# A fused encoder block on one core: operand tiles of the projections, gates and output projection placed 32 or 68 bytes apart

## The chip, the core and the metric

The kernel runs on one core of a Trainium2 chip. The metric is the time of one execution of the program on the device, in microseconds (us). Before the change three runs took 2656.34, 2660.68 and 2661.32 us; the median is 2660.68 us. The profiled execution, from which all rows below are taken, took 2661.26 us; its span from the first to the last instruction is 2659.4 us.

Engines are named as in the profile: PE is TensorE's matmuls, PEld its loads of the stationary operand, DVE VectorE, ACT ScalarE, POOL GpSimd, SP SyncE, which issues DMAs.

## The reference, cut to what matters

One layer, 2048 tokens, model width 1024, all in float32:

```python
n = rms_norm(h, g_mix)
z = n @ w_in + b_in                         # 1024 x 5120
q, k, v, u, bg, cg, ga, gc = split(z)       # 512 512 512 512 512 512 1024 1024
ya = chunked_rel_attention(q, k, v, ...)    # 8 heads x 64, bands of 576 keys
yc = bg * (conv_b + sum_j conv_w[j] * shift(cg * u, 2 - j))
m = sigmoid(ga) * (ya @ w_pa) + sigmoid(gc) * (yc @ w_pc)
h = h + m @ w_o
n2 = rms_norm(h, g_ffn)
h = h + hier_moe(n2, ...)                   # top group of 4, then top 2 of 8 SwiGLU experts
gate = sigmoid(rms_norm(h, g_ple) @ w_ple_gate + b_ple_gate)
h = h + gate * (p @ w_ple_proj)
```

## The kernel before

**Split products.** Every large product is made of three matmuls. An operand X is split into a high part, a rounded copy (`split`, line 79, on ACT), and a low part, X minus the high part (line 80, on DVE or POOL). `mm3` (lines 82 to 92) then issues, for each slice of 128 of the contraction, three matmuls into the same PSUM tile: stationary high with moving high (line 90), stationary high with moving low (line 91), stationary low with moving high (line 92). Each matmul is preceded by a load of its 128 x 128 stationary slice, so that the program on PE is a chain load, matmul, load, matmul. A stationary slice is 128 float32 of a partition, 512 bytes; a moving operand is 512 columns, 2048 bytes, or 256 columns, 1024 bytes.

**The stages, in order of time.** Stage 1 (0 to about 570 us) makes q, k and v of four heads at a time and, between their matmuls, the attention of earlier tiles. There the weights `wh`, `wl` (`load_w`, from line 161) are the moving operands, 512 columns for q and k and 256 for v, and the normalised tokens `nh`, `nl` the stationary ones. The weights of each half of the heads are 8 pairs of tiles, which stay for 16 tiles of tokens. Stage 2 (to about 1600 us) goes over four blocks of 512 tokens. For each it loads the tokens (`load_n`, 8 pairs `nh`, `nl`, moving), and streams the weights in chunks `whi`, `wlo` (stationary) through the projections u, C and B and the gates; `yh`, `yl` and `ych`, `ycl` are the moving operands of the products with w_pa and w_pc. `gate` gives 8 pairs `mh`, `ml`, which are stationary in the output projection (`out_proj`), where the chunks are the moving operand. Stage 3 (1630 to 2427 us) is the mixture of experts: gathered tokens `xAh`, `xAl`, `xB` and activations `aAh`, `aAl`, `aB` are stationary, weight chunks move. Stage 4 (2456 to 2655 us) is the last gate: `xh`, `xl` stationary, chunks `whi`, `wlo` and one pair `w7h`, `w7l` moving, 512 columns each, and for the last tile partly 256.

**Where tiles lie.** A pool lays its tiles out in a partition's memory one behind the other, each from a multiple of 32 bytes on; `bufs=8` under one name makes 8 equal buffers. Pools on the left start behind the constants of `setup`, whose last tile is a `pad`; pools on the right start from the other end. In this text the *place* of a tile is its first byte modulo 512. Since 128 float32 are 512 bytes and 512 columns are 2048, all slices of a tile that `mm3` uses begin at the place of the tile, and a moving operand also ends where the next row of 512 bytes has this place. *Place apart* is the place of the moving operand of a matmul less that of the stationary slice that is loaded for the next matmul while it runs.

The order of instructions on each engine is set by the order in which the code issues them; pools set which instruction waits for which buffer.

Of the kernel before, what the change touches and what calls it, by code (L numbers as in the profile page):

```python
# [7 lines left out]
F32 = mybir.dt.float32  # L8
F32R = mybir.dt.float32r
# [64 lines left out]
class K:  # L74
# [21 lines left out]
    def setup(self, ctx):  # L96
        tc, nc, a = self.tc, self.nc, self.a
        self.cst = c = ctx.enter_context(tc.tile_pool(name="cst", bufs=1))
        self.dr = d = ctx.enter_context(tc.tile_pool(name="dr", bufs=1, space=DRAM))
        self.ident = c.tile([128, 128], F32, name="ident")  # L100
        make_identity(nc, self.ident)
        self.identr = c.tile([128, 128], F32R, name="identr")
        nc.vector.tensor_copy(self.identr, self.ident)
        self.H = d.tile([S, D], F32, name="H")
        self.N2 = d.tile([S, D], F32, name="N2")
        self.Y = d.tile([2 * S + (NE + MAXOV) * CAP, D], F32, name="Y")
        self.PP = d.tile([S, D], F32, name="PP")
        self.mhalf = c.tile([128, 8], F32, name="mhalf")
        nc.vector.memset(self.mhalf, -0.5)
        self.NTd = d.tile([128, 8, S], F32, name="NTd")  # L110
        self.YAT = d.tile([128, 4, S], F32, name="YAT")
        self.banks, self.nbank = [], 0

        c.tile([128, 88], F32, name="pad")

    def bank(self, dt=F32):
        self.nbank += 1
# [9 lines left out]
    def stage1(self, outer, after, lead=11, lag=2):  # L127
        tc, nc, a = self.tc, self.nc, self.a
        with ExitStack() as ctx:
# [4 lines left out]
            pj = pjx.enter_context(tc.tile_pool(name="s1proj", bufs=2, side="right", reuse_waits="tile"))  # L134
# [25 lines left out]
            def load_w(g, ks):  # L160
                b = a["w_in"]
                for k in ks:
                    if g == 0:
                        raw = early[:, k - 4, 0:768] if k > 3 else att.tile([128, D], F32, name="QT", bufs=4)[:, 0:768]
                    else:
                        raw = pj.tile([128, D], F32, name="xt", bufs=3)[:, 0:768]
                    self.wlast = nc.sync.dma_start(raw.rearrange("p (s c) -> p s c", c=256),
                                      bass.AP(tensor=b.tensor, offset=b.offset + k * 128 * 5120 + g * 256,
                                              ap=[[5120, 128], [512, 3], [1, 256]]))
                    wh = pj.tile([128, 768], F32R, name="wh", bufs=8)  # L170
                    wl = pj.tile([128, 768], F32R, name="wl", bufs=8)
                    self.split(raw, wh, wl)
                    W[g, k] = (wh, wl)

# [64 lines left out]
            def proj(g, t):  # L239
# [4 lines left out]
                for half in range(2):  # L244
                    if g == 1 and t == 0:
                        load_w(g, range(4 * half, 4 * half + 4))
                    ks = range(4 * half, 4 * half + 4)
                    self.mm3(pqk, st[4 * half:4 * half + 4], [(W[g, k][0][:, 0:512], W[g, k][1][:, 0:512]) for k in ks], 4 * half, 8)
                    if half == 0:
                        yield  # L250
# [233 lines left out]
    def stage2(self, outer, inner):  # L484
# [30 lines left out]
        with ExitStack() as ctx:  # L515
            rctx = ctx.enter_context(ExitStack())
            rt = rctx.enter_context(tc.tile_pool(name="s2right", bufs=2, side="right", reuse_waits="tile"))
            bank = self.bank
            one = lambda shape, name: rt.tile(shape, F32, name=name, bufs=1)
            small = one([128, 128], "small")  # L520
            bT = small[:, 0:28]
            nc.scalar.dma_start(bT, a["b_in"][0, 1536:5120].rearrange("(c p) -> p c", p=128))
            cw = small[:, 28:40].rearrange("p (j c) -> p j c", j=3)
# [10 lines left out]
            def load_n(b):  # L534
                out = []
                for k in range(8):
                    raw = rt.tile([128, 512], F32, name="nraw")
                    nc.scalar.dma_start(raw, self.NTd[:, k, 512 * b:512 * b + 512])
                    hi = rt.tile([128, 512], F32R, name="nh", bufs=8)
                    lo = rt.tile([128, 512], F32R, name="nl", bufs=8)  # L540
                    self.split(raw, hi, lo)
                    out.append((hi, lo))
                return out
# [12 lines left out]
            def proj_T(ch, n, k0=0):  # L556

                ps = bank()
                K_ = len(n)
                st = [(ch[0][:, (k0 + k) * 128:(k0 + k + 1) * 128], ch[1][:, (k0 + k) * 128:(k0 + k + 1) * 128]) for k in range(K_)]  # L560
                self.mm3(ps, st, n, 0, K_)
                return ps
# [24 lines left out]
            def gate(c, n, ya, yc):  # L587
                pga = proj_T(self.chunk(), n)
                sa = two.tile([128, 512], F32, name="sa")
                nc.scalar.activation(sa, pga, AF.Sigmoid, bias=bT[:, 12 + c:13 + c])  # L590
                pgc = proj_T(self.chunk(), n)
                sc = two.tile([128, 512], F32, name="sc", bufs=1)
                nc.scalar.activation(sc, pgc, AF.Sigmoid, bias=bT[:, 20 + c:21 + c])
                ch = self.chunk()
                pa = proj_T(ch, ya)
                nc.vector.tensor_mul(sa, sa, pa)
                pc = proj_T(ch, yc, 4)
                nc.vector.tensor_mul(sc, sc, pc)  # L598
                nc.gpsimd.tensor_tensor(sa, sa, sc, op=ALU.add)  # L599
                hi = two.tile([128, 512], F32R, name="mh", bufs=8)  # L600
                lo = two.tile([128, 512], F32R, name="ml", bufs=8)
                self.split(sa, hi, lo)
                return hi, lo

# [155 lines left out]

            YC = []
            n = load_n(0)
            for c in range(4):
                for _ in conv(0, c, n):
# [3 lines left out]
            two = ctx.enter_context(tc.tile_pool(name="s2left", bufs=2, reuse_waits="tile"))  # L768
# [525 lines left out]
    def stage4(self, out):  # L1294
        tc, nc, a = self.tc, self.nc, self.a
        with ExitStack() as ctx:
            two = ctx.enter_context(tc.tile_pool(name="s4two", bufs=2, reuse_waits="tile"))
# [22 lines left out]
            def add(t, ys, h):  # L1320
                nc.vector.scalar_tensor_tensor(h, ys[0], self.WT[0][:, t:t + 1], h, op0=ALU.mult, op1=ALU.add)
                nc.vector.scalar_tensor_tensor(h, ys[1], self.WT[1][:, t:t + 1], h, op0=ALU.mult, op1=ALU.add)
# [53 lines left out]
            self.split_scaled(*w7, self.gple[:, 7:8])  # L1376
            WP = [self.chunk(6 - k) for k in range(7)] + [w7[1:]]
            order.close()
            two.tile([128, 48], F32, name="pad", bufs=1)
            add(todo[0], *ld[0][:2])  # L1380
            xs = turn(ld[0][1])
            r = norm(*ld[0][:2])
# [63 lines left out]
```

## Time and profile before

| | |
|---|---|
| median of three runs | 2660.68 us |
| profiled execution, its span | 2661.26 us, 2659.4 us |
| PE busy, share of the span, matmuls | 2595.2 us, 98%, 13313 |
| loads of the stationary operand (PEld) busy | 2184.5 us, 82% |
| DVE, ACT, POOL busy | 63%, 50%, 32% |
| granted TensorE clock, mean | 0.992 of full |

How to read the rows. The row of an engine on the page gives busy time, share of the span and instructions. A view by windows gives for each stretch its length, the busy time of each engine with the number of instructions, the granted TensorE clock, the share of the DMA engines and what they moved. A row of a group of instructions gives line, engine, operation, output<-inputs by the names in the code (stationary and moving in alphabetical order), the shapes, how many, the busy time in us and the mean duration of one in ns, and the idle time just before them. A row of the order of time gives the start in us, the duration, and the same names; a row with x4 stands for four in a run. Matmuls overlap in the profile: one starts well before the end of the one before it, so what a matmul costs is the distance from its start to the next start, here called the pace; in a settled chain the duration shown is the pace and about 162 ns.

### The profile page before, as it was taken

The page shows a single profiled execution, that of the slowest core. Times are in us where ns is not written, and L with a number is a line of the kernel's source. Part 1 is how long each engine was busy: PE and PEld are TensorE (multiplying, and loading weights), DVE is VectorE, ACT ScalarE, POOL GpSimd, SP SyncE. Part 2 cuts the span into 40 slices and gives each one's busy share as a digit, 9 for nine tenths or more (in the row PEclk, how much of TensorE's full clock was granted, in tenths as well). Part 3 has the DMA queues.
Part 4 walks back from the last instruction along what each step waited for, and adds up shares of the span by engine and source line. Part 5 has one row for each costly group of instructions (what it writes and reads, how often), then busy time and mean ns, then how long its engine had stood idle before and what let it go on. Part 6 is the DMA issues. An engine that isn't in the chain of part 4 may idle for free.

```text
span 2659.4 us, 36515 instructions
## 1 busy us (share of the span) xinstructions
PE 2595.2 (98%) x13313; PEld 2184.5 (82%) x13313; DVE 1675.8 (63%) x2399; ACT 1341.6 (50%) x2025; POOL 841.0 (32%) x681
## 2 busy tenths in 40 slices
PE   7999999999999999999999998999999999998999
PEld 6898888878888888888888886888888888886887
DVE  7778867775444445444445446777777678775654
ACT  5666755564333323332333224766666666665322
POOL 2655465510000100010001003544554555542222
PEclk9999999999999999999999998999999999998999
DMA  5222311044335334533453346888989889987553
GB/s 185 72 68 60 110 48 41 9 129 137 102 128 189 103 95 143 170 102 95 137 170 103 95 151 210 307 309 295 315 304 313 302 314 309 312 309 258 207 187 103
DMA packets 349623, 465.11 MB, mean 175 GB/s; under 512 B 26240, under 2 KB 222080, under 8 KB 349440
## 3 DMA queue, kind: packets, MB, share of 16 engines
q1 hardware_dynamic: 314944, 388.35, 44.8%
q0 software_dynamic: 12096, 43.00, 4.3%
q10 hardware_dynamic: 22400, 31.41, 3.5%
q8 instruction: 105, 1.72, 0.3%
q14 instruction: 78, 0.64, 0.1%
HBM read 400.30 MB, written 62.39 MB: 174 GB/s over the span
## 4 chain that ended last, share of the span: by engine, by line
PE 84%; DVE 6%; DMA 4%; issue 3%; POOL 1%; ACT 1%; SPq 0%; another core or an unknown queue 0%; DVEq 0%; POOLq 0%; ACTq 0%
PE acc L90 22%; PE acc L92 22%; PE acc L91 22%; PE acc L1039 4%; PE acc L1040 4%; PE big L348 2%; PE big L380 2%; DMA h<-H 1%; DMA wraw<-w 1%; PE acc L393 1%; PE acc L394 1%; PE acc L1008 1%; PE acc L674 1%; PE acc L294 1%; POOL g L1362 1%
## 5 line engine op out<-in xcount | busy, mean ns | idle before, releaser
L80 DVE TENSOR_TENSOR wlo<-wraw,whi 128x1024 fp32r<-128x1024 f32 x464 | 694.5, 1509 | 478.4 <-ACT whi L79 465.3
L79 ACT CAST whi<-wraw 128x1024 fp32r<-128x1024 f32 x560 | 585.8, 1053 | 777.8 <-PE acc L91 375.6
L90 PE MATMUL acc<-nh,whi 128*128 128x512 f32 x896 | 349.7, 392 | 2.0 <-ACT nh L79 2.0
L91 PE MATMUL acc<-nl,whi 128*128 128x512 f32 x896 | 350.0, 391 | 0.0
L92 PE MATMUL acc<-nh,wlo 128*128 128x512 f32 x896 | 348.8, 389 | 0.0
L80 POOL TENSOR_TENSOR wlo<-wraw,whi 128x1024 fp32r<-128x1024 f32 x96 | 238.1, 2480 | 123.4 <-ACT whi L79 115.8
L599 POOL TENSOR_TENSOR sa<-sa,sc 128x512 f32<-128x512 f32 x32 | 41.3, 1290 | 538.3 <-DVE sc L598 493.2
L90 PE MATMUL acc<-whi,xAh 128*128 128x512 f32 x512 | 204.1, 399 | 0.4 <-ACT xAh L1011 0.4
L91 PE MATMUL acc<-wlo,xAh 128*128 128x512 f32 x512 | 200.1, 391 | 0.0
L92 PE MATMUL acc<-whi,xAl 128*128 128x512 f32 x512 | 200.0, 391 | 0.0
L90 PEld LDWEIGHTS acc<-nh,whi 128*128 128x128 f32 x896 | 168.1, 188 | 37.2 <-ACT nh L79 2.7
L92 PEld LDWEIGHTS acc<-nh,wlo 128*128 128x128 f32 x896 | 168.3, 188 | 34.5
L91 PEld LDWEIGHTS acc<-nl,whi 128*128 128x128 f32 x896 | 168.3, 188 | 33.4
L90 PE MATMUL acc<-wh,nh 128*128 128x512 f32 (+1 forms) x512 | 176.6, 346 | 0.3 <-ACT wh L79 0.2
L91 PE MATMUL acc<-wl,nh 128*128 128x256 f32 (+1 forms) x512 | 174.1, 341 | 2.1 <-DVE wl L80 2.1
L92 PE MATMUL acc<-wh,nl 128*128 128x256 f32 (+1 forms) x512 | 174.5, 342 | 0.0
L385 ACT CAST PTh<-big 128x640 fp32r<-128x640 f32 (+4 forms) x128 | 80.3, 628 | 85.7 <-PE big L380 84.3
L367 ACT ACTIVATE L<-L,mn 128x640 f32<-128x640 f32 (+4 forms) x128 | 98.4, 769 | 38.2 <-DVE mn L365 15.1
L90 PEld LDWEIGHTS acc<-whi,xAh 128*128 128x128 f32 x512 | 96.5, 189 | 20.8 <-ACT xAh L1011 1.0
L92 PEld LDWEIGHTS acc<-whi,xAl 128*128 128x128 f32 x512 | 96.3, 188 | 20.5 <-DVE xAl L1012 0.2
L1039 PE MATMUL acc<-whi,xB 128*128 128x512 f32 x288 | 112.9, 392 | 0.0
L1040 PE MATMUL acc<-wlo,xB 128*128 128x512 f32 x288 | 112.2, 390 | 0.0
(328 smaller groups left out, 5918.1 us busy)
## 6 DMA issues: line engine op xcount, KB each, us to landing
wraw<-w SPq DMA_DIRECT2D x384, 512.0 KB
wraw<-w_in SPq DMA_DIRECT2D x112, 512.0 KB
wraw<-w_o SPq DMA_DIRECT2D x32, 512.0 KB
y<-Y SPq DMA_DIRECT2D x32, 512.0 KB
xt<-x SPq DMA_DIRECT2D x16, 512.0 KB
xt<-NTd SPq DMA_DIRECT2D x16, 512.0 KB
nraw<-NTd ACTq DMA_DIRECT2D x32, 256.0 KB
wraw<-w_pa SPq DMA_DIRECT2D x32, 256.0 KB
```

What stands on the lines that cost most here:

```text
L79: (hi_eng or self.nc.scalar.copy)(hi, raw)
L80: (lo_eng or self.nc.vector).tensor_sub(lo, raw, hi.bitcast(F32))
L90: self.nc.tensor.matmul(ps, sh, mh, start=first, stop=False)
L91: self.nc.tensor.matmul(ps, sh, ml, start=False, stop=False)
L92: mm = self.nc.tensor.matmul(ps, sl, mh, start=False, stop=last)
L348: nc.tensor.matmul(big[:, 512 * c:512 * c + hi - lo], QT[g, t][:, s, h * 128:(h + 1) * 128], KT[0][:, h, ks:ks + hi - lo], start=(s == 0), ...
L367: nc.scalar.activation(L[:, :n], L[:, :n], AF.Exp, bias=mn, scale=-1.0, accum_out=sm)
L380: nc.tensor.transpose(pt[:, j * 128:(j + 1) * 128], L[:, j * 128:(j + 1) * 128], self.ident)
L385: nc.scalar.copy(hi, ptv)
L599: nc.gpsimd.tensor_tensor(sa, sa, sc, op=ALU.add)
L1039: nc.tensor.matmul(ps, st, ch[0][:, sl], start=first, stop=False)
L1040: nc.tensor.matmul(ps, st, ch[1][:, sl], start=False, stop=last)
```

## The change

No operation, DMA or wait is taken out or put in. In stage 1 and 2 the names of operand tiles get a number, so that each of 8 pairs has tiles of its own with one buffer instead of one of 8 buffers of a common name; each tile is 8 float32 wider than what is used of it, so that the next one begins 32 bytes further on. The tiles `mh`, `ml` are in addition used from element c on, so that successive pairs are 68 bytes apart. The pad behind the constants gets 256 bytes smaller, and so does the tile `small`; a pad in stage 4 goes.

```diff
-        c.tile([128, 88], F32, name="pad")
+        c.tile([128, 24], F32, name="pad")
...
-                    wh = pj.tile([128, 768], F32R, name="wh", bufs=8)
-                    wl = pj.tile([128, 768], F32R, name="wl", bufs=8)
+                    wh = pj.tile([128, 776], F32R, name=f"wh{k}", bufs=1)[:, 0:768]
+                    wl = pj.tile([128, 776], F32R, name=f"wl{k}", bufs=1)[:, 0:768]
...
-            small = one([128, 128], "small")
+            small = one([128, 64], "small")
...
-                    hi = rt.tile([128, 512], F32R, name="nh", bufs=8)
-                    lo = rt.tile([128, 512], F32R, name="nl", bufs=8)
+                    hi = rt.tile([128, 520], F32R, name=f"nh{k}", bufs=1)[:, 0:512]
+                    lo = rt.tile([128, 520], F32R, name=f"nl{k}", bufs=1)[:, 0:512]
...
-                hi = two.tile([128, 512], F32R, name="mh", bufs=8)
-                lo = two.tile([128, 512], F32R, name="ml", bufs=8)
+                hi = two.tile([128, 520], F32R, name=f"mh{c}", bufs=1)[:, c:c + 512]
+                lo = two.tile([128, 520], F32R, name=f"ml{c}", bufs=1)[:, c:c + 512]
...
-            two.tile([128, 48], F32, name="pad", bufs=1)
```

All instructions stand in the same order as before on every engine; only a few waits of DVE and POOL sit one instruction earlier or later. The places that the two built programs give to the operands (bytes modulo 512; k and c from 0 to 7):

| stage: moving with stationary | before | after |
|---|---|---|
| 1: `wh`, `wl` with `nh`, `nl` | 288 with 288 | `wh` 288 + 64k, `wl` 320 + 64k, with 288 |
| 1: `KT` with `QT`; `PTh`, `PTl` with `Vt` | 0 (or 256) with 0; 0 with 0 | all 256 more |
| 2: `nh`, `nl` with `whi`, `wlo` | 0 with 0 | `nh` 64k, `nl` 64k + 32, with 0 |
| 2: `yh`, `yl` with `whi`, `wlo` | 256 with 0 | 0 with 0 |
| 2: `ych`, `ycl` with `whi`, `wlo` | 0 with 0 | 0 with 0 |
| 2: `whi`, `wlo` with `mh`, `ml` | 0 with 256 | 0 with `mh` 68c, `ml` 68c + 32 |
| 3: `whi`, `wlo` with `xAh`, `xAl`, `xB`, `aAh`, `aAl`, `aB` | 0 with 0 | 0 with 256 |
| 4: `whi`, `wlo`, `w7h`, `w7l` with `xh`, `xl` | 0 with 192 | `whi`, `wlo` 0, `w7h`, `w7l` 256, with 256 |

## Rows read from the trace of the kernel before

**Rows 1.** The page, busy time of engines over the span.

```profile
PE 2595.2 (98%) x13313; PEld 2184.5 (82%) x13313; DVE 1675.8 (63%) x2399; ACT 1341.6 (50%) x2025; POOL 841.0 (32%) x681
```

**Rows 2.** The page, the chain that ended last.

```profile
PE 84%; DVE 6%; DMA 4%; issue 3%; POOL 1%; ACT 1%; SPq 0%; another core or an unknown queue 0%; DVEq 0%; POOLq 0%; ACTq 0%
```

**Rows 3.** Windows by stage: 1, 2, 3 and 4.

```profile
0.00:570.00 570.00, 533.59 (x3606) 480.60 (x3607) 442.44 (x923) 359.37 (x735) 297.66 (x298) 0.99 0.24 75
...
640.00:1594.00 954.00, 952.62 (x4442) 792.78 (x4440) 450.34 (x606) 325.21 (x413) 72.02 (x93) 1.00 0.41 130
...
1630.00:2427.00 797.00, 792.77 (x3762) 650.68 (x3761) 591.40 (x554) 531.54 (x666) 393.70 (x208) 0.99 0.88 303
...
2456.00:2655.00 199.00, 197.08 (x938) 162.89 (x936) 106.97 (x134) 60.55 (x106) 51.91 (x58) 1.00 0.51 173
```

**Rows 4.** Groups of matmuls by form, the whole span.

```profile
L90 PE MATMUL acc<-nh,whi 128*128 128x512 f32 x896 | 349.7, 392 | 2.0 <-ACT nh L79 2.0
...
L90 PE MATMUL acc<-wh,nh 128*128 128x512 f32 x256 | 103.2, 403 | 0.3 <-ACT wh L79 0.2
...
L90 PE MATMUL acc<-whi,mh 128*128 128x512 f32 x256 | 99.9, 390 | 0.0
...
L90 PE MATMUL acc<-wh,nh 128*128 128x256 f32 x256 | 73.9, 289 | 0.0
```

**Rows 5.** Order of time on PE, stage 2, a settled chain of projections, ends only.

```profile
648.84 0.39 PE L92 MATMUL acc<-nh,wlo 128*128 128x512 f32 x1
...
652.24 0.39 PE L92 MATMUL acc<-nh,wlo 128*128 128x512 f32 x1
```

**Rows 6.** Order of time on PE, stage 2, output projection, ends only.

```profile
800.04 0.39 PE L90 MATMUL acc<-whi,mh 128*128 128x512 f32 x1
...
803.44 0.39 PE L90 MATMUL acc<-whi,mh 128*128 128x512 f32 x1
```

**Rows 7.** Order of time on PE, stage 4, the gate, ends only.

```profile
2500.58 0.39 PE L90 MATMUL acc<-whi,xh 128*128 128x512 f32 x1
...
2509.51 0.39 PE L90 MATMUL acc<-w7h,xh 128*128 128x512 f32 x1
```

**Rows 8.** Groups of matmuls by form, the whole span, those of stage 4.

```profile
L90 PE MATMUL acc<-whi,xh 128*128 128x512 f32 x217 | 86.2, 398 | 1.8 <-ACT xh L1341 1.8
L92 PE MATMUL acc<-whi,xl 128*128 128x512 f32 x217 | 85.2, 394 | 0.0
...
L91 PE MATMUL acc<-wlo,xh 128*128 128x512 f32 x217 | 84.7, 390 | 0.0
...
L90 PE MATMUL acc<-w7h,xh 128*128 128x512 f32 x31 | 12.1, 392 | 0.0
...
L90 PE MATMUL acc<-whi,xh 128*128 128x256 f32 x14 | 3.9, 279 | 0.0
```

**Rows 9.** Order of time on PE, stage 1, ahead of four score matmuls.

```profile
117.35 0.40 PE L92 MATMUL acc<-wh,nl 128*128 128x512 f32 x1
117.58 0.75 PE L348 MATMUL big<-KT,QT 128*128 128x320 f32 x4
118.17 0.49 PE L380 MATMUL big<-ident,L 128*128 128x128 f32 x3
```

**Rows 10.** One group by form, the instant 117.10 us.

```profile
L90 PE MATMUL acc<-wh,nh 128*128 128x512 f32 x1 | 0.4, 389 | 0.0
```

**Rows 11.** One group by form, the instant 117.56 us.

```profile
L92 PE MATMUL acc<-wh,nl 128*128 128x512 f32 x1 | 0.4, 396 | 0.0
```

**Rows 12.** Order of time on PE, stage 1, the v part, ends only.

```profile
106.19 0.28 PE L92 MATMUL acc<-wh,nl 128*128 128x256 f32 x1
...
107.15 0.28 PE L91 MATMUL acc<-wl,nh 128*128 128x256 f32 x1
```

**Rows 13.** Order of time on PE, stage 4, last tile, 256 columns, ends only.

```profile
2649.53 0.28 PE L91 MATMUL acc<-wlo,xh 128*128 128x256 f32 x1
...
2652.36 0.28 PE L91 MATMUL acc<-wlo,xh 128*128 128x256 f32 x1
```

## The prediction

> **What bounds the kernel now.** I read the page's busy times first: PE is busy for 2595.2 of 2659.4 us, 98%, and no other engine over 63% (PEld, its own loads, aside) [rows 1]. The chain that ended last says the same from the other end: 84% of it is PE; DVE has 6%, DMA 4% [rows 2]. The windows by stage show that this holds where the change is made: in stage 2 PE is busy 952.6 of 954.0 us at a granted clock of 1.00, in stage 4 197.1 of 199.0, in stage 1 533.6 of 570 [rows 3]. So in these stages a nanosecond more or less from one matmul's start to the next's goes straight into the end, and nothing else can. In stage 3 DMA is 88% busy [rows 3], but PE still 792.8 of 797.
>
> The question is then what the pace of a matmul is, and whether the places of its operands enter it. In a settled chain of stage 2, 15 matmuls of 512 columns take from 648.84 to 652.24 us: 226.7 ns each [rows 5]. At the full clock, 2.4 GHz, 512 columns are 213.3 ns; so each carries 13.3 ns on top. In the v part of stage 1 with 256 columns, 8 take 0.96 us, 120.0 ns each [rows 12], against 106.7: again 13.3 ns. The top is thus a cost per pair of load and matmul, not per column. All these chains have moving and stationary operand at equal places. The output projection has them 256 bytes apart, and its 15 matmuls take 3.40 us, 226.7 ns as well [rows 6]. The one chain in which they are otherwise apart is stage 4, with 320 (64 beyond 256): 39 matmuls from 2500.58 to 2509.51 us, 229.0 ns each [rows 7], 2.3 ns more. Its groups show where: durations of 398 (some of them restarts of a chain) and 394 ns in lines 90 and 92, 390 in line 91 [rows 8], against 389 to 392 in stage 2 [rows 4]. The same stage's 256 columns go the other way: 24 in 2.83 us, 117.9 ns each, 2.1 ns less than 120.0 [rows 13, 12]. So places do enter the pace, by about 2 ns, with either sign.
>
> **The change part by part.** No instruction comes or goes, so each term is a number of matmuls times a change of pace. The sum is made against the profiled 2661.26 us, which lies 0.6 us above the median of the runs.
>
> What becomes of the places apart: in stage 2's projections the moving operand is at 64k (high) or 64k + 32 (low) with stationary slices at 0, so a matmul's place apart is 64k in lines 90 and 92 and 64k + 32 in line 91. Of the 24 matmuls of a projection, 4 (lines 90 and 92 at k = 0 and 4) stay 0 or 256 apart, 12 come to even multiples of 32, and 8 to odd ones. Stage 1 has the same pattern, the output projection one like it.
>
> Price of an even multiple: the row of stage 4, +2.3 ns for 512 columns and -2.1 ns for 256 [rows 7, 12, 13].
>
> Price of an odd multiple: no chain of the trace has one. The nearest row is a single matmul of stage 1, `wh` at 288, while a slice of `QT` at 0 is loaded, 288 apart: it lasts 396 ns where the one of a settled chain just before lasts 389 [rows 10, 11], +7 ns; with the four score matmuls behind it the stretch to 118.17 us takes 0.82 us, and at 13.3 ns each on top it would be 226.7 + 4 x 146.7 = 813 ns [rows 9], so most of the 7 ns stays. That is a step from one place to another, not a steady pace, so I bound the price by -2.1 from below (the one gain that the rows show) and 7 from above, and take 4.6, half way between the even price and this row, to which it is the nearest in kind.
>
> Stage 2, projections: 3 x 896 = 2688 matmuls [rows 4]. Low: 896 x 4.6 = 4.1 us. High: 1792 less the quarter at equal places, 1344 x 2.3 = 3.1 us. Together +7.2.
>
> Stage 2, output projection: 3 x 256 [rows 4]; 256 with a low slice to load x 4.6 = 1.2, 7/8 of 512 x 2.3 = 1.0. Together +2.2. That `mh`, `ml` now start at multiples of 4 bytes instead of 32 has no row at all; I put nothing on it, since a load of the stationary slice ends before the matmul beside it does.
>
> Stage 1, q and k: 3 x 256 of 512 columns [rows 4]: 256 x 4.6 + 384 x 2.3 = 1.2 + 0.9 = +2.1. Here chains are short and often interrupted (403 ns mean against 389 [rows 4, 10]), which may hide some of it. The v part, 3 x 256 of 256 columns: 640 not at equal places x -2.1 = -1.3.
>
> Stage 4 goes from 320 to 256 apart, `w7h` to 0: its 744 matmuls (217 and 31 in each of the three lines [rows 8]) come to the pace of rows 6: 744 x -2.3 = -1.7; the 42 of 256 columns (14 in each line [rows 8]) x +2.1 = +0.1.
>
> At nothing: `yh`, `yl` come from 256 to 0 apart, stage 3 from 0 to 256; both paces are 226.7 ns [rows 5, 6]. `KT`, `QT`, `PTh`, `PTl`, `Vt` keep their places to one another. One buffer for each of eight numbered names is the same ring as eight of one name, used in the same order, so no wait is added. DVE and ACT write the same bytes to other places; if that slowed them, stage 2 has DVE idle for half and ACT for two thirds of it [rows 3].
>
> Sum: 7.2 + 2.2 + 2.1 - 1.3 - 1.7 + 0.1 = +8.6 us, 2661.3 to 2669.9 in a profile and 2669.3 beside the median of the runs: 2669 us.
>
> A rule of the Trainium skill speaks against any effect. SBUF — State Buffer, section "SBUF: two separate sides", says that among the engines only the port pair of VectorE and GpSimd is contended and that TensorE never waits on anyone. The trace does not quite bear that out: 229.0 against 226.7 ns for the same instructions at other places. By the rule the sum would be nothing, the third case below. TensorE: Matmul & The Clock Gate, section "Back-to-back issue gap", gives a lone matmul 2.5 ns on top of its columns, where the trace has 13.3 with a load beside each. An estimate from that page: if staggering freed every matmul that leaves its equal place of all but this, 4200 x 10.8 ns would be 45 us.
>
> **The rivals.**
>
> Faster, because two reads collide at equal places. The 13.3 ns are there only with a load beside the matmul, and load and matmul start within a few ns of each other at equal places; if they hit the same part of the memory, moving one of them away lets both pass. It decides as soon as the mean price over the places is below zero. For it speaks the -2.1 ns of 256 columns [rows 12, 13]; against it that 256 apart gives exactly 226.7 as 0 does, and that 64 beyond is worse. Number of matmuls that leave equal places: 2240 + 704 + 640 + 640 = 4224; at -2.1 ns each -8.9, with stage 4's -1.6 -10.5 us: 2650 us. If all of the 13.3 went, which no row shows, 56 us: 2604.
>
> No change: the paces of stage 4 come from its mix of work, not from places, or the sixteen places cancel. For it: signs differ between 512 and 256 columns. Against: stage 4's 39 matmuls are a steady chain at the full clock. Time: 2658 to 2664.
>
> Slower by more: every change of place costs the 7 ns of rows 11, since a chain in which each matmul has another place never settles. (2240 + 704 + 640) x 7 = 25.1, less 1.3 and 1.6: +22 us, 2683.
>
> **How the numbers follow.** Slower by the even and odd prices, with the last rival as its far end: 0.47, from 2665 (odd places at the even price: 896 + 256 + 256 matmuls x 2.3 less, 3.2 us off the sum) to 2683. Faster: 0.30, mostly 2645 to 2655. No change: 0.23. What a measurement of this kernel tells from no change is 0.2%, 5.3 us. Of the first case 0.04 falls within that, of the second 0.01: faster 0.29, within 0.28, slower 0.43. The likeliest case gives the time, 2669, with 2665 to 2683 as its own range; the whole range goes from 2640, which leaves a tenth for a large gain, to 2684.
>
> **What would show it.** Right: in stage 2 the durations of lines 90 to 92 with `nh`, `whi` rise from 389 to 392 towards 393 to 396, line 91 most; `mh` likewise; in stage 4 `xh` falls to 390; the v part falls below 120 ns; stage 2 gets about 9 us longer, stage 4 1.6 shorter. Wrong: means of those lines under 388, or a pace of 226.7 throughout. It would also be wrong if DVE or ACT casts of the shifted tiles got longer and PE began to wait for them.

## The result and the profile after

The changed kernel is slower. Four runs took 2675.83 to 2684.11 us, median 2678.80, beside 2659.94 us for the kernel before; the ratio is 1.0075, 95% interval 1.0055 to 1.0095, or 15 to 25 us. The forecast was 2669 us with a range of 2640 to 2684: the direction and the place of the loss were right, its size, 8.6 us where the medians differ by 18.9, less than half. The profiled execution, the fastest of the four, took 2675.83 us with a span of 2674.0, 14.6 us more than before.

The page of the kernel after, busy times and the chain that ended last:

```profile
PE 2608.0 (98%) x13313; PEld 2179.9 (82%) x13313; DVE 1690.7 (63%) x2399; ACT 1337.4 (50%) x2025; POOL 835.2 (31%) x681
...
PE 87%; DVE 5%; DMA 4%; issue 2%; ACT 2%; POOL 1%; another core or an unknown queue 0%; ACTq 0%; DVEq 0%; POOLq 0%; SPq 0%
```

PE has as many matmuls as in [rows 1] and is busy for 12.8 us longer; its share of the chain grows from 84% [rows 2] to 87%. The windows by stage, same stretches as [rows 3]:

```profile
0.00:570.00 570.00, 531.69 (x3616) 476.84 (x3617) 444.32 (x927) 360.18 (x738) 297.09 (x298) 0.99 0.25 76
...
640.00:1594.00 954.00, 953.31 (x4342) 779.86 (x4341) 445.32 (x599) 320.49 (x406) 70.71 (x90) 1.00 0.41 128
1630.00:2427.00 797.00, 791.01 (x3758) 649.22 (x3758) 607.25 (x579) 525.45 (x661) 392.75 (x208) 0.99 0.88 301
2456.00:2655.00 199.00, 194.36 (x907) 161.16 (x908) 107.38 (x129) 65.53 (x115) 52.18 (x62) 0.98 0.57 193
```

The last stretch holds fewer matmuls because the stage begins 16 us later, and stages 1 and 3 hold nearly as many as before. In the 954 us of stage 2 PE is as fully busy and as fast clocked as before, but gets through 4342 matmuls instead of 4442. So nothing new is waited for; each matmul takes longer. Where the stage begins and ends shows how much; first matmul of the projections and last of the output projection, before and then after:

```profile
568.62 0.50 PE L90 MATMUL acc<-nh,whi 128*128 128x512 f32 x1 [0.52 <-ACT nh L79]
...
1591.19 0.39 PE L92 MATMUL acc<-whi,ml 128*128 128x512 f32 x1
```

```profile
566.71 0.50 PE L90 MATMUL acc<-nh,whi 128*128 128x512 f32 x1 [1.49 <-ACT nh L79]
...
1607.23 0.39 PE L92 MATMUL acc<-whi,ml 128*128 128x512 f32 x1
```

That is 1022.6 us before and 1040.5 after, +17.9. Stage 1 ends 1.9 us earlier, what lies between stage 2 and stage 4 is 0.3 shorter, stage 4 1.2: 17.9 - 1.9 - 0.3 - 1.2 = 14.5.

The groups by form after, which answer to [rows 4] and [rows 8]:

```profile
L91 PE MATMUL acc<-nl,whi 128*128 128x512 f32 x896 | 354.7, 396 | 0.0
L90 PE MATMUL acc<-nh,whi 128*128 128x512 f32 x896 | 352.8, 395 | 3.1 <-ACT nh L79 3.1
L92 PE MATMUL acc<-nh,wlo 128*128 128x512 f32 x896 | 352.4, 393 | 0.0
...
L90 PE MATMUL acc<-wh,nh 128*128 128x512 f32 x256 | 103.1, 403 | 0.8 <-ACT wh L79 0.8
...
L90 PE MATMUL acc<-whi,mh 128*128 128x512 f32 x256 | 101.5, 397 | 0.0
...
L92 PE MATMUL acc<-whi,xl 128*128 128x512 f32 x217 | 84.6, 390 | 0.0
...
L90 PE MATMUL acc<-wh,nh 128*128 128x256 f32 x256 | 73.3, 286 | 0.0
...
L90 PE MATMUL acc<-yh,whi 128*128 128x512 f32 x128 | 50.4, 393 | 0.0
```

The projections rise from 392 to 395 in line 90, from 391 to 396 in line 91; the output projection from 390 to 397; `xl` falls from 394 to 390, the v part from 289 to 286. Two things were not expected: the products with `yh`, forecast at their old pace, stand at 393, and the output projection rises more than the projections. The row of the products with `yh` before:

```profile
L90 PE MATMUL acc<-yh,whi 128*128 128x512 f32 x128 | 49.8, 389 | 0.0
```

The paces after, each from the first and the last start of a chain: 15 steps in the projections, 15 in the output projection, and 39 in stage 4:

```profile
648.70 0.40 PE L92 MATMUL acc<-nh,wlo 128*128 128x512 f32 x1
...
652.17 0.39 PE L92 MATMUL acc<-nh,wlo 128*128 128x512 f32 x1
...
799.15 0.40 PE L90 MATMUL acc<-whi,mh 128*128 128x512 f32 x1
...
802.64 0.39 PE L90 MATMUL acc<-whi,mh 128*128 128x512 f32 x1
...
2515.33 0.39 PE L90 MATMUL acc<-whi,xh 128*128 128x512 f32 x1
...
2524.17 0.39 PE L90 MATMUL acc<-whi,xh 128*128 128x512 f32 x1
```

231.3 ns against 226.7 [rows 5], 232.7 against 226.7 [rows 6], 226.7 against 229.0 [rows 7]. Below, the *top* of a matmul is the distance from its start to the next start less its columns at 2.4 GHz (213.3 ns for 512, 106.7 for 256), averaged over a group without restarts of a chain (tops over 30 ns):

| group | matmuls | top before | after | in us |
|---|---|---|---|---|
| projections, `nh`, `nl` | 2688 | 13.7 | 18.1 | +11.8 |
| output projection, `mh`, `ml` | 768 | 13.5 | 19.6 | +4.6 |
| products with `yh`, `ych` | 768 | 13.4 | 14.9 (`yh` 16.4, `ych` 13.4) | +1.2 |
| q and k, 512 columns | 768 | 15.3 | 18.3 | +2.3 |
| v, 256 columns | 768 | 12.5 | 11.0 | -1.1 |
| stage 4, 512 columns | 744 | 15.7 | 13.7 | -1.5 |

The three groups of stage 2 make 17.6 us of its 17.9. The rest is in the output projection too: 16 of its matmuls after the change have 40 to 42 ns on top, 14 of them at the same two spots of a chain, and are no restarts. With them the group rises by 4.9 us. One of them, to the next start:

```profile
790.48 0.42 PE L92 MATMUL acc<-whi,ml 128*128 128x512 f32 x1
790.73 0.40 PE L90 MATMUL acc<-whi,mh 128*128 128x512 f32 x1
```

### The profile page after: what moved, and what is told of

Read it like the earlier page. It is cut to its first block, busy times and chain, and to the rows that moved or that the text cites. A ratio compares the mean times of both kernels' runs of the same rounds, so it can differ in the third digit from the quotient of the medians.

```text
span 2674.0 us, 36516 instructions
## 1 busy us (share of the span) xinstructions
PE 2608.0 (98%) x13313; PEld 2179.9 (82%) x13313; DVE 1690.7 (63%) x2399; ACT 1337.4 (50%) x2025; POOL 835.2 (31%) x681
## 4 chain that ended last, share of the span: by engine, by line
PE 87%; DVE 5%; DMA 4%; issue 2%; ACT 2%; POOL 1%; another core or an unknown queue 0%; ACTq 0%; DVEq 0%; POOLq 0%; SPq 0%
PE acc L90 23%; PE acc L91 23%; PE acc L92 23%; PE acc L1039 3%; PE acc L1040 3%; DMA wraw<-w 2%; PE big L348 2%; PE big L380 2%; PE acc L393 1%; PE acc L394 1%; PE acc L674 1%; PE acc L1008 1%; DMA h<-H 1%; PE acc L294 1%; DVE PTl L386 1%
## 5 line engine op out<-in xcount | busy, mean ns | idle before, releaser
L80 DVE TENSOR_TENSOR wlo<-wraw,whi 128x1024 fp32r<-128x1024 f32 x464 | 710.6, 1544 | 475.1 <-ACT whi L79 463.7
L91 PEld LDWEIGHTS acc<-wlo,xAh 128*128 128x128 f32 x512 | 96.5, 189 | 19.8 <-POOL wlo L80 1.1
```

Source lines behind the costliest of these rows:

```text
L80: (lo_eng or self.nc.vector).tensor_sub(lo, raw, hi.bitcast(F32))
L91: self.nc.tensor.matmul(ps, sh, ml, start=False, stop=False)
```

## The experiments

Theories at the start: S, the loss comes from the place apart changing from matmul to matmul, so that a chain never settles (the forecast's rival "slower by more"); P, each place apart has its own price (the forecast's view); F, the starts at multiples of 4 bytes cost in the output projection.

**One place for all.** `nh`, `nl` all at 352, `mh`, `ml` all at 384:

```diff
-            small = one([128, 128], "small")
+            small = one([128, 64], "small")
...
                     lo = rt.tile([128, 512], F32R, name="nl", bufs=8)
+                    if b == k == 0:
+                        rt.tile([128, 40], F32, name="padp", bufs=1)
...
+                if c == 0 and n is n0:
+                    two.tile([128, 32], F32, name="pade", bufs=1)
                 hi = two.tile([128, 512], F32R, name="mh", bufs=8)
...
```

> In stage 2 all eight pairs `nh`, `nl` stand at one place, 352, instead of 0, and all pairs `mh`, `ml` at 384 instead of 256; so every matmul of the projections is 352 apart and every one of the output projection 128. Everything else is as in the kernel before. Theory S (settling): what costs in the changed kernel is that the place apart differs from one matmul to the next, so that a chain never comes to its steady pace; at one constant place it does, at 226.7 to 229.0 ns, and the time is that of before or up to 3456 x 2.3 ns = 8 us more. Theory P (price of the place): each place apart has a price of its own whatever stands beside it; in the changed kernel the matmuls at 352 carry 22.8 ns on top of their columns, against 13.7 in the kernel before, and those at 128 19.1 against 13.5; so 2688 x 9.1 + 768 x 5.6 ns = +29 us, some 2689 us.

Measured: median 2683.00 us, ratio 1.0079 (1.0063 to 1.0095), as slow as the changed kernel. Its groups and the ends of stage 2:

```profile
L92 PE MATMUL acc<-nh,wlo 128*128 128x512 f32 x896 | 355.3, 396 | 0.0
L91 PE MATMUL acc<-nl,whi 128*128 128x512 f32 x896 | 355.0, 396 | 0.0
L90 PE MATMUL acc<-nh,whi 128*128 128x512 f32 x896 | 354.7, 397 | 0.7 <-ACT nh L79 0.7
...
567.02 0.79 PE L90 MATMUL acc<-nh,whi 128*128 128x512 f32 x1 [0.71 <-ACT nh L79]
...
1611.75 0.39 PE L92 MATMUL acc<-whi,ml 128*128 128x512 f32 x1
```

Stage 2 takes 1044.7 us, 22.2 more than before and 4 more than with sixteen places. (The profiled execution is this kernel's fastest of four, and in it what lies between stage 2 and stage 4 is 5.6 us shorter than before, so that its whole is only 13.3 us longer.) The chain does settle: its tops repeat 23.7, 17.7, 18.7 from one matmul to the next, a mean of 20.0, and the whole group is at 20.1. Theory S falls as the main cause. P holds in kind, with a smaller size: the matmuls at 352 had 22.8 in the changed kernel and have 20.0 in a settled chain of their own, so what a place costs also depends on the places beside it. The output projection at 128 apart has 19.1, as P expected.

**Two places in turn.** `nh` at 352, `nl` at 384, `mh` at 0, `ml` at 32, by pads like those above:

```diff
                     hi = rt.tile([128, 512], F32R, name="nh", bufs=8)
+                    if b == k == 0:
+                        rt.tile([128, 8], F32, name="padq", bufs=1)
                     lo = rt.tile([128, 512], F32R, name="nl", bufs=8)
...
```

> In stage 2 all `nh` stand at 352 and all `nl` at 384, all `mh` at 0 and all `ml` at 32: two places that take turns, 32 bytes apart, instead of sixteen. Theory S: two of three steps of the projections change the place by 32, which is less than in the changed kernel, where nearly every step does and every third by 64 as well; of the 4.4 ns per matmul there between a third and all remains, +4 to +12 us in the projections and +1 to +4 in the output projection: 2665 to 2676 us, and a pace that is steady in a cycle of three. Theory P: two thirds of the projections at 352 (22.8 ns on top in the changed kernel) and a third at 384 (16.6) are 20.7 against 13.7, 2688 x 7.0 ns = +19 us; the output projection at 0 and 480 is not far from the changed kernel's +4.6: some 2683 us.

Measured: 2677.40 us, ratio 1.0062 (1.0044 to 1.0079). The projections have 20.0 ns on top, the output projection 20.0 (17.0 at 0 apart, 25.8 at 480). The ends of stage 2:

```profile
567.31 0.50 PE L90 MATMUL acc<-nh,whi 128*128 128x512 f32 x1 [1.33 <-ACT nh L79]
...
1610.86 0.39 PE L92 MATMUL acc<-whi,ml 128*128 128x512 f32 x1
```

Stage 2 takes 1043.6 us, 21.0 more than before. In the projections P expected 20.7 ns, and S at most 13.7 + 4.5 = 18.2. The time alone does not decide: 2677 us lies between S's 2676 and P's 2683, and in this profile what lies between stage 2 and stage 4 is 3.8 us shorter than before.

**`mh`, `ml` without the shift of c elements.**

```diff
-                hi = two.tile([128, 520], F32R, name=f"mh{c}", bufs=1)[:, c:c + 512]
-                lo = two.tile([128, 520], F32R, name=f"ml{c}", bufs=1)[:, c:c + 512]
+                hi = two.tile([128, 520], F32R, name=f"mh{c}", bufs=1)[:, 0:512]
+                lo = two.tile([128, 520], F32R, name=f"ml{c}", bufs=1)[:, 0:512]
```

> The changed kernel, but `mh`, `ml` start at the beginning of their tiles, at 64c and 64c + 32, and no longer c elements further on at 68c. If it is the starts that are not multiples of 32 bytes that cost in the output projection (theory F), its 768 matmuls fall from 19.6 ns on top of their columns to the 18.1 of the projections or below, and the time by 1 to 4.6 us: 2672 to 2676 us with the kernel after at about 2677. Theories S and P: no difference to the changed kernel beyond 1 us, since the places apart change as before.

Measured: 2676.70 us, ratio 1.0053 (1.0037 to 1.0068); the output projection at 19.0 instead of 19.6 ns, 0.4 us. The 16 matmuls with 40 to 42 ns on top are gone, another 0.4 us. Stage 2 takes 1039.2 us, 1.3 less than in the changed kernel; the interval of the time overlaps that of the change. By the tops F accounts for 0.8 of 4.9 us.

**Stage 4 alone, 256 apart.**

```diff
-            two.tile([128, 48], F32, name="pad", bufs=1)
+            two.tile([128, 64], F32, name="pad", bufs=1)
```

> The kernel before with one edit: the pad in stage 4 is 64 instead of 48 columns wide, so that `xh`, `xl` stand at 256 instead of 192 and the moving operands 256 apart from them instead of 320. If the change's gain in stage 4 comes from this place and not from what runs ahead of it, the 744 matmuls of 512 columns fall from 15.7 ns on top to about 13.6 and the time by 1.5 us; the 42 of 256 columns rise from 11.2 to about 13.2, +0.1. Together -1.4 us, 2658.5 us: less than the runs can tell in their medians, but visible in the group means of stage 4 (395 and 398 ns in lines 92 and 90 towards 390 to 392). If the gain were the work of a later start or of another kernel's state, nothing would change.

Measured: 2660.65 us, ratio 0.9991 (0.9978 to 1.0004). The top falls as expected, 15.7 to 13.7, but the group means do not (399 and 394 ns) and the stage is 200.9 us long instead of 199.3. Its windows, its wait, and DVE in the order of time:

```profile
2456.90:2600.00 143.10, 143.10 (x678) 119.30 (x677) 80.32 (x97) 48.65 (x85) 38.56 (x45) 1.00 0.60 204
2600.00:2623.60 23.60, 20.48 (x95) 16.11 (x95) 11.51 (x14) 5.89 (x11) 4.90 (x7) 1.00 0.31 110
2623.60:2628.00 4.40, 4.40 (x14) 3.46 (x13) 2.10 (x4) 1.10 (x2) 1.71 (x2) 0.61 0.64 221
...
PE acc L90 <- ACT xh L1341: 3.1, 2, 1.9
...
2603.66 1.28 DVE L1321 SCALAR_TENSOR_TENSOR h<-y,WT,h 128x1024 f32<-128x1024 f32 x1 [6.35 <-DMA h<-H]
```

Up to 2600 us the saving is there: 678 matmuls in 143.1 us, where the kernel before has 680 in 144.8. Then PE has caught up with the chain that makes `xh` of the next tile: DVE stood idle 6.35 us for the transfer of `h`, and PE waits 3.1 us in two pieces (1.8 us, once, in the kernel before). After the second wait the granted clock of a stretch of 4.4 us is 0.61; PE in the order of time there:

```profile
2622.20 0.50 PE L90 MATMUL acc<-whi,xh 128*128 128x512 f32 x1 [1.85 <-ACT xh L1341]
...
2625.00 0.63 PE L92 MATMUL acc<-whi,xl 128*128 128x512 f32 x1
2625.43 0.63 PE L90 MATMUL acc<-whi,xh 128*128 128x512 f32 x1
```

These start 0.43 us apart, twice 213.3 ns: the level of 1.2 GHz. So in this execution 1.5 us won in the pace came back as waiting and as a lower clock. The lower clock does not belong to the places: it followed one wait of 1.8 us for `xh` in the run without staggered `nh`, `nl` too, but none followed a wait of 1.8 us in the kernel before and one of 1.9 us in the run with `mh`, `ml` unshifted. The waiting does seem to: of nine profiles of the layer, the five with stage 4 at 0 or 256 apart wait 1.8 to 4.4 us for `xh` there, and the stage takes 197.6 to 201.1 us; the four at 320 apart wait 0.5 to 1.8 us, and it takes 197.5 to 199.3. The faster pace does not make the stage shorter.

**The change without its staggered `nh`, `nl`.**

```diff
-                    hi = rt.tile([128, 520], F32R, name=f"nh{k}", bufs=1)[:, 0:512]
-                    lo = rt.tile([128, 520], F32R, name=f"nl{k}", bufs=1)[:, 0:512]
+                    hi = rt.tile([128, 512], F32R, name="nh", bufs=8)
+                    lo = rt.tile([128, 512], F32R, name="nl", bufs=8)
```

> The changed kernel with one part undone: `nh`, `nl` of stage 2 are again 512 columns wide, so that all of them stand at 0, equal with the stationary slices; the staggered `wh`, `wl` and `mh`, `ml` stay. By the map of places the 2688 matmuls of the projections go back from 18.1 ns on top of their columns to 13.7, 11.8 us, and the 768 of the products with `yh`, `ych` from 14.9 to 13.4, 1.2 us, although their places don't change, because a chain that follows one at equal places needs no time to settle: 13 us less than the changed kernel, about 4.3 us more than before, 2664 to 2665 us. If the staggered tiles cost through DVE and ACT, which write them, and not through the distance of the two operands, the stage keeps part of its loss and the products of `yh` keep their 14.9 ns.

Measured: 2668.72 us, ratio 1.0024 (1.0011 to 1.0036), 6.4 us above the kernel before where 4.3 was expected, and 0.5% or 13.6 us less than the change, by the two ratios.

```profile
569.16 0.50 PE L90 MATMUL acc<-nh,whi 128*128 128x512 f32 x1 [1.48 <-ACT nh L79]
...
1596.42 0.39 PE L92 MATMUL acc<-whi,ml 128*128 128x512 f32 x1
...
L90 PE MATMUL acc<-yh,whi 128*128 128x512 f32 x128 | 49.8, 389 | 0.0
```

Stage 2 takes 1027.3 us: 4.7 more than before, which is about the output projection's 4.9. The products with `yh` are back at 389 ns, with unchanged places. They lost in the changed kernel because of the chain ahead of them; the run with one place for all has the same, 16.5 ns on top for `yh` at the old 256 apart. Where it is lost shows in the changed kernel, in 12 matmuls with `yh`, directly behind a projection, and the 12 with `ych` behind them; first, ninth and last:

```profile
679.39 0.40 PE L90 MATMUL acc<-yh,whi 128*128 128x512 f32 x1
...
681.24 0.39 PE L92 MATMUL acc<-yh,wlo 128*128 128x512 f32 x1
...
684.64 0.39 PE L92 MATMUL acc<-ych,wlo 128*128 128x512 f32 x1
```

The first eight take 231 ns each, the fifteen behind them 226.7: coming back to equal places costs about eight matmuls, and then the chain has settled. This is the part of theory S that holds.

**A map of places.** Chains alone, with the whole layer left out, so that nothing but PE runs:

```diff
+        def chain(name, at, cols, times, s=0):
+            with tc.tile_pool(name="ps" + name, bufs=2, space=PSUM) as ps:
+                for _ in range(times):
+                    acc = ps.tile([128, 512], F32, name=name)[:, 0:cols]
+                    k.mm3(acc, stat(s), [tuple(v[:, p // 4:p // 4 + cols] for v, p in zip(mv[i], at(i))) for i in range(8)], 0, 8)
...
+        for d in range(16):
+            chain("d" + "abcdefghijklmnop"[d], lambda i: (32 * d, 32 * d), 512, 3)
```

> Not the layer: only chains of the product's three matmuls, with stationary slices at 0 and moving operands at a chosen place, and nothing else running on the chip beside PE once the operands are loaded. Per place apart 72 matmuls of 512 columns at 0, 32, ..., 480, then 72 of 256 columns at each, then 512 columns at 4, 8, 16, 36 and 68; then the steps of the changed kernel (64k and 64k + 32, `step`), both operands at 160 (`both`), the stationary at 160 and the moving one at 0 (`other`, 352 apart), 24 at 352 and 24 at 256 in turn (`far`, `near`), and 352 and 384 as in the kernel with two places (`turn`). Theory P (each place apart has its price, and it is the distance of the two operands that counts): the chains at 0 and 256 carry 13.3 to 13.7 ns on top of their columns, 320 15.7, 352 about 20, 128 about 19; the mean over the sixteen is near the 18.1 ns of the changed kernel's projections, and so is `step`; `both` is at 13.3, `other` at about 20. Theory A (the absolute place decides, rows of 512 bytes that an operand crosses): `both` is at 16 or more, and `other` unlike 352. Theory W (the price is a collision with what DVE, ACT and DMA write meanwhile): all chains are at 13.3 to 14, `step` too. If a chain takes some matmuls to come to its pace (theory S as an addition to P), `near` lies 2 to 4 ns above the chain at 256.

A window over most of the chains, in which no engine but PE works, and groups by form: `da` is 0 apart, `dd` 96, `dl` 352, `other` 352 with the stationary operand moved instead, `both` 0 with both at 160, `step` the change's own sequence; `ea` and `eg` are 0 and 192 with 256 columns:

```profile
36.00:550.00 514.00, 511.82 (x2725) 430.92 (x2724) 0.00 (x0) 0.00 (x0) 0.00 (x0) 1.00 0.00 1
...
L92 PE MATMUL dd<-nh,wlo 128*128 128x512 f32 x24 | 9.6, 399 | 0.0
L92 PE MATMUL dl<-nh,wlo 128*128 128x512 f32 x24 | 9.6, 399 | 0.0
L92 PE MATMUL other<-nh,wlo 128*128 128x512 f32 x24 | 9.6, 399 | 0.0
...
L91 PE MATMUL step<-nl,whi 128*128 128x512 f32 x24 | 9.5, 395 | 0.0
...
L92 PE MATMUL da<-nh,wlo 128*128 128x512 f32 x24 | 9.3, 389 | 0.0
...
L92 PE MATMUL both<-nh,wlo 128*128 128x512 f32 x24 | 9.3, 389 | 0.0
...
L92 PE MATMUL ea<-nh,wlo 128*128 128x256 f32 x24 | 6.8, 283 | 0.0
...
L92 PE MATMUL eg<-nh,wlo 128*128 128x256 f32 x24 | 6.6, 276 | 0.0
```

The tops in ns, from the starts of the last 24 matmuls of each chain:

| place apart | 0 | 32 | 64 | 96 | 128 | 160 | 192 | 224 |
|---|---|---|---|---|---|---|---|---|
| 512 columns | 13.3 | 20.0 | 15.6 | 20.0 | 19.4 | 21.1 | 20.0 | 20.0 |
| 256 columns | 13.2 | 10.0 | 11.1 | 13.3 | 13.3 | 10.5 | 6.7 | 11.7 |

From 256 to 480 the values repeat to 0.2 ns, so the period is 256 bytes. `both` is at 13.3 and `other` at 20.0: at 160, the one other place tried for the stationary slices, it is the distance that counts, and theory A falls. The map has all of the loss with DVE, ACT and DMA at rest, and `step` has 18.1 ns, the changed kernel's projections to the tenth; from the seventh matmul of a projection on, its tops follow theirs one by one to within 1 ns. Theory W falls. On S the map says nothing: `near`, the chain at 256 behind one at 352, comes to 13.3 ns after 5 to 11 matmuls with tops of 11 to 23 ns, but each chain of the map begins with a pause of some 120 ns, and the chain at 256 behind its own kind takes as many. Places of 4, 36 and 68 have 23.3, 21.3 and 26.7.

**A finer map**, in steps of 4 bytes, by the same function:

```diff
+        for x in range(64):
+            chain("u" + abc[x // 4] + abc[x % 4], lambda i: (4 * x, 4 * x), 512, 2)
```

> Not the layer: chains alone, as in the map before, but in steps of 4 bytes over one period of 256 (names u.. with 512 columns, v.. with 256), 48 matmuls each, and in steps of 32 with 320, 384 and 128 columns (w, x, y). The first map has, for 512 columns, 13.3 ns on top at 0, 15.6 at 64, 18.3 at 16 and 19.4 to 23.3 elsewhere. If the price follows the row of memory that both reads are in, it falls in steps of 32 or 64 bytes and no place is under 13.3; if it follows the distance itself, it is lowest at single places, and one of the 64 may be at 6.7 or below, as 192 is with 256 columns.

For 512 columns the lowest top is 13.3, at 0, 28, 60, 156, 236 and 252; the highest 26.7, at 20, 100, 120, 132 and 244. So equal places are as good as any, and the kernel before has them in all but stage 4. The price doesn't fall in steps of 32 or 64, so it is not set by the row both reads are in. A distance of 68, at 26.7 in the first map, has 23.3 here. At the output projection's own distances in the changed kernel the tops of this map average 19.5, where the kernel has 19.6. With 256 columns 112 and 192 have 6.7, and 8 has the most, 20.0; with 320 columns seven of eight places have 13.3, one 13.5; with 384 they have 13.3 to 16.7. With 128 columns all eight places have 58.3: there the place does not matter.

**A map by width of the load.**

```diff
+        for n, w in (("w", 128), ("x", 96), ("y", 64), ("z", 32)):
+            for x in range(8):
+                chain(n + abc[x], lambda i: (32 * x, 32 * x), 512, 2, 0, w)
```

> Not the layer: chains of 48 matmuls of 512 columns at the places 0 to 224 in steps of 32, with stationary slices of 128 (names w..), 96 (x), 64 (y) and 32 columns (z), so that the load beside each matmul reads 512, 384, 256 and 128 bytes of a partition. Theory C (the matmul's stream loses time to the load's read beside it, and the distance sets how often the two meet): what is on top of the 213.3 ns falls with the width of the load, from 20 ns at 32, 96 and 160 and 13.3 at 0 towards a fourth or a third of it with 32 columns, and the places come closer to one another. Theory Q (a fixed time for each pair of load and matmul, which depends on the places alone): the four widths give the same 13.3, 20, 15.6, 20, 18.8 to 19.4, 21, 20, 20 ns.

At 0 apart 128, 96, 64 and 32 columns of load give 13.3, 16.7, 16.7 and 18.3 ns, at 192 apart 20.0, 15.0, 19.4 and 18.3. The top does not fall with the bytes that the load reads, and is not fixed by the place alone: both theories fall. It was also seen that one place can have more than one steady cycle: 128 apart came out at 19.4, 18.8 and 20.0 in the three maps, and the 256-column matmuls of stage 4, all at 320 apart, have 11.2 ns on top in the kernel before and with one place for all, but 6.7 with two places.

**A version from the map.** v part and the products with `Vt` at 192 apart, stage 4 at 256:

```diff
-                    wh = pj.tile([128, 768], F32R, name="wh", bufs=8)
-                    wl = pj.tile([128, 768], F32R, name="wl", bufs=8)
-                    self.split(raw, wh, wl)
+                    wh = pj.tile([128, 512], F32R, name="wh", bufs=8)
+                    wl = pj.tile([128, 512], F32R, name="wl", bufs=8)
+                    self.split(raw[:, 0:512], wh, wl)
+                    if (g, k) == (0, 0):
+                        pj.tile([128, 48], F32, name="padv", bufs=1)
+                    vh = pj.tile([128, 256], F32R, name="vh", bufs=8)
+                    vl = pj.tile([128, 256], F32R, name="vl", bufs=8)
+                    self.split(raw[:, 512:768], vh, vl)
...
+                    att.tile([128, 16], F32, name="padt", bufs=1)
                 Vt = att.tile([128, 4, 2, HD], F32R, name="Vt", bufs=8)
...
```

> The kernel before with places chosen from the map: 512 columns stay at equal places, matmuls of 256 columns go to 192 apart, where the map has 6.7 ns on top of their columns against 13.2 at 0. For this the weights of v get tiles of their own, `vh`, `vl`, 192 bytes from `nh` (`wh`, `wl` keep q and k), `Vt` moves by 64 bytes so that `PTh`, `PTl` are 192 from it, and stage 4 has its operands 256 apart. If the map holds in the kernel: the v part 768 matmuls from 12.5 to about 7 ns, -4.2 us; the products with `Vt` (627 records) from 12.3 to about 8, as their chains are short, -2.7 us; stage 4 -1.4 us; together -8.3 us, about 2652 us. Stage 1 waits for DVE and ACT for part of its time (PE busy 533.6 of 570 us), so a third to a half of its 6.9 us may turn into waiting: 2652 to 2656 us. Against it: 32 splits more on ACT and on DVE, since q and k and v are split apart, which at the start of the stage could cost 1 to 2 us. If the low price at 192 were an effect of chains with nothing beside them, only the -1.4 us of stage 4 remain.

Measured: 2659.29 us, ratio 0.9993 (0.9982 to 1.0005): no difference that can be told. The tops fall (v part 12.5 to 9.1, products with `Vt` 12.3 to 9.9; that they stay above 6.7 because their chains are short is not shown), and stage 2 begins at 564.1 instead of 568.6 us; but stage 4 takes 201.1 us, with waits for `xh` of 4.4 us in three pieces.

**The same without the edit in stage 4:**

```diff
-            two.tile([128, 64], F32, name="pad", bufs=1)
+            two.tile([128, 48], F32, name="pad", bufs=1)
```

> The kernel with `vh`, `vl` and `PTh`, `PTl` at 192 apart, but stage 4 as in the kernel before, 320 apart. In the run with both edits stage 2 began 4.5 us earlier than in the kernel before (564.1 against 568.6 us), while stage 4 took 201 us instead of 199: its matmuls were 1.5 ns each faster, but PE waited up to 2 us, three times, for `xh` of the last tiles, which wait for the transfer of `h`. If the gain of stage 1 reaches the end and stage 4's waits come from its faster pace: stage 2 begins at 563 to 565 us again, stage 4 takes 197 to 199 us, and the time is 4 to 6 us under before, about 2656 us with before at 2661. If the waits of stage 4 come and go with the transfers, whatever its pace: 0 to 4 us under before.

Measured: 2659.49 us, ratio 0.9995 (0.9983 to 1.0006). The tops of stage 1 are nearly as low as in the run before (9.4 and 10.0), yet stage 2 begins at 566.5 us; stage 4 takes 198.5. The gain in stage 1 is 2 us here, 4.5 there, and kernels with an unchanged stage 1 begin stage 2 between 567.0 and 569.9: it is below what these runs can tell. No version beats the kernel before by a measurable amount.

## Why the prediction was right in direction and short in size

**What bounds.** Right for stage 2: PE stays the bound, no wait is added, and the loss is that stage's alone. That a nanosecond of pace goes straight into the end did not hold in stages 1 and 4, as shown below.

**Projections: +7.2 forecast, +11.8 measured.** This is the term that was mis-sized, by its price per place. Means of the changed kernel, over 13.7: odd multiples of 32 +5.6 ns (forecast 4.6), even multiples +3.9 (forecast 2.3), equal places +3.1 (forecast 0). 896 x 5.6 + 1344 x 3.9 + 448 x 3.1 = 11.6 us. The even price came from the only other place that the trace had, stage 4's 320; the map shows that this is 64 in a period of 256, the cheapest multiple of 32 after 0 (15.6), and the other even places have 19.4 to 20.0. The odd price was taken too low: the row of 396 against 389 ns, discounted as a single step, was 288 apart, which is 32 in a period of 256, and the map has 20.0 there in a steady chain, 6.7 over 13.3. The gap at equal places is what was left of theory S: coming back to 0 apart from another place costs several matmuls, and here the chain stays for one. Prices per place give the sum, not the single matmul: weighted by how often the projections use each place, the map's tops average 18.1, as measured, but in the changed kernel equal places have 16.9 (13.3 in the map), 192 has 17.4 (20.0) and 96 has 22.0 (20.0). The sum and the signs of the forecast did not fit each other either: durations that rise by 4 ns over 2688 matmuls, as it expected and as came about, are 10.8 us and not 7.2.

**Output projection: +2.2 forecast, +4.9 measured**, by the same price. Putting nothing on the 4-byte starts is 0.8 us of this, by the run without the shift.

**Products with `yh`, `ych`: nothing forecast, +1.2 measured.** Their places were judged by themselves, not by the chain ahead of them. All of it is in `yh`, which stands directly behind a projection; with `nh` at equal places it is back.

**Stage 1.** q and k +2.3 (forecast +2.1) and v -1.1 (-1.3) in the pace were right, but neither reaches the end: the three kernels with staggered `wh` begin stage 2 at 566.7, 568.4 and 569.2 us, the four with equal places there at 568.6, 567.0, 567.3 and 569.9. Stage 1's waits take up what the pace gives or takes.

**Stage 4: -1.7 forecast, -1.5 measured** in the pace. The stage is 1.2 us shorter, but three kernels that leave it as it was have it 0.8 to 1.8 us shorter too, and the run with this edit alone 1.6 us longer: a gain in the length is not shown.

**The rivals.** "Slower by more" came nearest in time, 2683 us, but its cause is the lesser part: one place for all, with nothing that changes from matmul to matmul, costs no less time than sixteen, and 4 us more in stage 2. "Faster" fell for 512 columns and is half right for 256; its premise, that the 13.3 ns are there only with a load beside the matmul, no run here shows, since in every kernel and map each matmul has its load. "No change" fell. The forecast had tied it to the rule by which TensorE never waits on anyone (the Trainium skill, SBUF — State Buffer, section "SBUF: two separate sides"). The runs do not speak against that rule: the map has 13.3 to 26.7 ns on top with no other engine at work, so what is slow lies between PE's own load and matmul, which the rule does not speak of. That there would be no effect did not follow from it.

What sets the price of a distance stays open. It is not the absolute place, not other engines, not the row of memory, and it does not fall with the bytes that the load reads. The starts show chains that lock into cycles of a few matmuls, and which cycle depends on distance, columns, width of the load and what ran ahead.

## What to carry to other kernels

Where a load and a matmul run side by side for thousands of matmuls, the distance of the two operands modulo 256 bytes was worth up to 13 ns each here: measure it as a map of bare chains, one run for all places, before moving tiles. Equal places are the floor for 512 columns in these maps; padding to spread tiles over the memory cost 0.75% here. One other place in the trace is not a price for all others, a chain's pace depends on the chain ahead of it as well, and a faster pace is only a gain in a stage whose next operand is already there.

## What the runs showed of the hardware

- The time from one 512-column matmul to the next, with a 128-column load between, depends on the distance of the operands with a period of 256 bytes: 226.7 ns at 0, 228.9 at 64, 232.1 to 234.4 at the other multiples of 32, 240.0 at 68 in one map and 236.7 in another.
- With 256 columns 113.3 ns at 192 apart, against 119.9 at 0; with 128 columns 111.7 ns at all of eight places.
- At 0 or 256 apart a chain needs 5 to 11 matmuls after a pause to come to its cycle, and about eight directly behind a chain at other places. A place can have more than one steady cycle: 128 apart has 18.8, 19.4 and 20.0 ns over the columns in three maps.
- A wait of 1.85 us of PE in stage 4 was followed by a stretch of 4.4 us with a mean granted clock of 0.61, in which matmuls started 0.43 us apart. A wait of 1.8 us in the same stage of the kernel before was not: the clock stayed at 1.00.
